# Cross entropy of 256 rows: the first 64 rows read as groups of 16 and 48 rows in place of 8 and 56

## The chip, the cores and the metric

The kernel runs on one core of one Trainium2 chip. The metric is the device time of one execution in microseconds (us). A core has five engines that run side by side and wait for each other through semaphores: TensorE (PE in the profile), VectorE (DVE), ScalarE (ACT), GpSimd (POOL) and SyncE (SP). Here SP does nothing but issue transfers from DRAM; the transfers themselves run on 16 DMA engines. The on-chip memory has 128 partitions, and every compute instruction works on all partitions at once, along the columns of a tile.

## The reference

```python
def setup_inputs():
    batch, num_classes = 256, 32000
    return {
        "logits": np.random.randn(batch, num_classes).astype(np.float32),
        "labels": np.random.randint(0, num_classes, size=batch).astype(np.int32),
    }

def reference(logits, labels):
    log_probs = logits - np.max(logits, axis=-1, keepdims=True)
    log_probs = log_probs - np.log(np.sum(np.exp(log_probs), axis=-1, keepdims=True))
    return np.array([-log_probs[i, labels[i]] for i in range(batch)]).astype(np.float32)
```

For each row the result is log(sum of exp(x)) - x[label]. The logits are 256 x 32,000 floats, 32.77 MB, and every one of them has to be read once and go through one exponential.

## The kernel before

The 256 rows are cut into five groups (`GROUPS`, line 18: 8, 56, 128, 32 and 32 rows). The rows of one group lie one behind the other in DRAM, so a group is one contiguous stretch; `flat` (line 142) cuts this stretch into 128 equal runs, and run p goes to partition p. A group of k rows gives k x 250 columns in each partition. Each group is fetched in one or several loads, cut by columns (`LOADS`, line 20); each load is one transfer issued by SP (`load`, line 213).

Group 0 has 8 rows. It is one load of 2,000 columns, 1 MB, and partition p holds a sixteenth of row p // 16. Group 1 has 56 rows in one load of 14,000 columns: 56 rows don't divide 128 partitions, so a partition's run reaches over row borders, and only pieces of 2,000 columns, seven to a partition, belong to one row each. `span` and `parts` (lines 135 and 136) work this out: with k rows, the run of a partition is cut into k / gcd(k, 128) parts, and 128 / gcd(k, 128) such parts make a row.

`exps` (line 217) runs one exponential on ScalarE for each part of a load, in place. For the loads of the first two groups it also leaves the sum over the columns of each part in `near`. For most later loads (`HALVED`) ScalarE only takes the exponential, and VectorE adds the two halves of the tile and accumulates the sum (line 315).

The sums of a row's pieces lie in different partitions. TensorE adds them: `products` (line 231) multiplies each column of `near` with a 128 x k matrix of weights (`weigh`) that holds, for each row, exp(-x[label]) in the partitions which belong to it and zero elsewhere. The masks `holds` of these partitions are made on GpSimd, with a memset and two selections for each group (lines 274 to 285). The values exp(-x[label]) come from an indirect transfer by the labels (line 268), an exponential on ScalarE placed directly behind load 1's (`GATHERED = 1`, line 290), and a spread over all partitions by TensorE (line 295). VectorE then makes the weights, one product for each part of each group (line 301). The logarithm of a group's row of sums (`logs`, line 239) is the result.

Memory is the reason for the order of loads. There are six slots for loads 0 to 5, whose transfers SP issues one behind the other; the first of them is moved ahead of the barrier at the start of the program. Loads 6 and 7 use the slots of loads 2 and 3 again, so SP waits for VectorE's sums of these. The six loads of the last group, from 2,496 columns down to 608, lie side by side in the slot of load 1. SP issues strictly in this order. ScalarE takes the loads in the order of their numbers. The logarithm of the first two groups stands behind load 2's exponential.

Of the kernel before, what the change touches and what calls it, by code (L numbers as in the profile page):

```python
# [14 lines left out]
AF = mybir.ActivationFunctionType  # L15


GROUPS = [8, 56, 128, 32, 32]

LOADS = [  # L20
    [2000],
    [14000],
    [8896, 8192, 8320, 6592],
    [4736, 3264],
    [2496, 1824, 1344, 992, 736, 608],
# [94 lines left out]
def kernel(  # L120
# [9 lines left out]
    B, C = logits.shape  # L130
    assert B == P * ROWS == sum(GROUPS)
    row_at = [sum(GROUPS[:g]) for g in range(len(GROUPS) + 1)]


    span = [P // math.gcd(k, P) for k in GROUPS]
    parts = [k // math.gcd(k, P) for k in GROUPS]
    for k, ns, n, m in zip(GROUPS, LOADS, span, parts):
        assert sum(ns) * P == k * C and C % n == 0
# [4 lines left out]
        logits[row_at[g]:row_at[g + 1], :].rearrange("k c -> (k c)").rearrange("(p n) -> p n", p=P)  # L143
        for g in range(len(GROUPS))
    ]
# [224 lines left out]
```

## Time and profile before

| | us |
|---|---|
| median of 3 runs (82.7 to 82.85) | 82.72 |
| the profiled execution, its time | 82.85 |
| the profiled execution, its span (first to last instruction) | 81.2 |
| ScalarE busy | 58.5 |
| VectorE busy | 28.5 |
| TensorE busy | 13.0 |
| GpSimd busy | 6.4 |
| bytes moved, mean rate over the span | 32.77 MB, 404 GB/s |

The transfers, as the page lists them: load 1 is the one of 7,000 KB and lands 20.8 us after its issue, load 0 the one of 1,000 KB, with 5.0 us. Loads 2 to 5 are those of 4,448, 4,096, 4,160 and 3,296 KB, with 30.9, 40.1, 49.3 and 56.6 us from issue to landing. All are issued within the first 3.3 us, so these times are mostly time in the queue.

How to read the views: L222 is the exponential, L315 VectorE's sum, L215 the issue of a load, L234 the products of TensorE, L240 the logarithm. ACT is ScalarE and SPq the queue of SP. In the row of slices each character is one fortieth of the span and gives the busy share in tenths. A wait in brackets stands ahead of the instruction that had to wait, with what released it.

### The profile page before, as it was taken

The numbers are of one execution on the slowest core, as the hardware profiler recorded it, in microseconds if no ns is written. First come the engines' busy times: TensorE is split into PE (matmuls) and PEld (weight loads), VectorE is DVE, ScalarE is ACT, GpSimd is POOL, SyncE is SP. The second block draws the span as 40 slices with busy tenths as digits, with TensorE's granted clock in tenths as the row PEclk, the third lists the DMA queues.
The fourth block names the chain that finished last, engine by engine and source line by source line (L and its number), as shares of the span: only waits on it lengthen the run. The fifth ranks groups of instructions, "written<-read, shape, count | busy, mean of one in ns | idle before, by whom it ended". The sixth has DMA issues, their size and how long they took to land.

```text
span 81.2 us, 322 instructions
## 1 busy us (share of the span) xinstructions
PE 13.0 (16%) x80; PEld 7.7 (10%) x80; DVE 28.5 (35%) x37; ACT 58.5 (72%) x35; POOL 6.4 (8%) x22
## 2 busy tenths in 40 slices
PE   0040000000000000067000020020000201159971
PEld 0040000000000000046000000000000000035640
DVE  1010000000000000026019926950099198898870
ACT  6054000000399999999999993599979999999993
POOL 4006982000000000000000000000000000000000
DMA  4999899999989898998998998999999999999930
GB/s 91 532 407 414 386 441 442 441 442 441 491 351 508 368 508 357 436 500 355 436 508 361 443 492 360 416 429 455 392 420 429 426 431 420 423 424 415 405 150 1
DMA packets 2084, 32.77 MB, mean 404 GB/s; under 512 B 290, under 2 KB 291, under 8 KB 1060
## 3 DMA queue, kind: packets, MB, share of 16 engines
q1 hardware_dynamic: 2018, 32.77, 94.8%
q0 software_dynamic: 64, 0.00, 0.1%
q10 hardware_dynamic: 2, 0.00, 0.0%
HBM read 32.77 MB, written 0.00 MB: 404 GB/s over the span
## 4 chain that ended last, share of the span: by engine, by line
DMA 61%; ACT 34%; SPq 2%; another core or an unknown queue 1%; issue 1%; PE 0%
DMA x<-in_logits_dram 61%; ACT x L222 24%; ACT x_tail L222 9%; SPq L215 2%; PE bank L234 0%; ACT res L240 0%
## 5 line engine op out<-in xcount | busy, mean ns | idle before, releaser
L222 ACT ACTIVATE x<-x 128x2000 f32<-128x2000 f32 (+6 forms) x14 | 49.2, 3525 | 20.6 <-DMA x<-in_logits_dram 20.6
L315 DVE SCALAR_TENSOR_TENSOR x<-x 128x4448 f32<-128x4448 f32 (+5 forms) x6 | 21.8, 3631 | 14.1 <-ACT x L222 14.1
L292 DVE TENSOR_SCALAR diag<-ident,eg 128x128 f32<-128x128 f32 x2 | 0.5, 282 | 28.8 <-ACT eg L290 28.8
L234 PE MATMUL bank<-weights,near 128*1 128x32 f32 (+3 forms) x40 | 5.2, 270 | 32.6 <-DVE x L315 31.1
L222 ACT ACTIVATE x_tail<-x_tail 128x2496 f32<-128x2496 f32 (+5 forms) x6 | 7.5, 1302 | 0.0
L295 PE MATMUL bank<-diag,ones 128*128 128x128 f32 x4 | 1.2, 462 | 29.3 <-DVE diag L292 29.3
L312 PE MATMUL bank<-diag,x 128*1 128x128 f32 x32 | 5.8, 368 | 0.0
L234 PEld LDWEIGHTS bank<-weights,near 128*1 128x1 f32 x40 | 2.4, 94 | 35.5 <-DVE x L315 33.4
L315 DVE SCALAR_TENSOR_TENSOR x_tail<-x_tail 128x1248 f32<-128x1248 f32 (+3 forms) x4 | 4.1, 1024 | 0.6 <-ACT x_tail L222 0.3
L295 PEld LDWEIGHTS bank<-diag,ones 128*128 128x128 f32 x4 | 0.9, 323 | 29.4 <-DVE diag L292 29.4
L312 PEld LDWEIGHTS bank<-diag,x 128*1 128x1 f32 x32 | 3.5, 112 | 2.1
L268 POOL DMA_INDIRECT g_at<-in_logits_dram,idx x2 | 2.1, 1030 | 0.6 <-issue 0.3
L207 ACT ACT_TABLE_LOAD x1 | 1.3, 1283 | 0.8 <-PEq L354 0.8
L301 DVE TENSOR_TENSOR weights<-holds,bank 128x56 f32<-128x56 f32 (+3 forms) x11 | 1.4, 204 | 1.2 <-PE bank L295 1.2
L257 PE MATMUL bank<-one,lbl_row 1*128 1x1 f32 x4 | 1.0, 352 | 4.9 <-DVE lbl_row L255 4.9
L255 DVE CAST lbl_row<-words 1x256 f32<-1x256 int32 x1 | 0.3, 281 | 3.5 <-DMA words<-in_labels_dram 3.5
L282 POOL TENSOR_SCALAR_AFFINE_SELECT holds<-holds 128x32 f32<-128x32 f32 (+3 forms) x5 | 1.5, 292 | 0.3
L222 ACT ACTIVATION_READ_ACCUMULATOR x<-x 128x1 f32 x8 | 1.5, 186 | 0.0
L278 POOL TENSOR_SCALAR_AFFINE_SELECT holds<-holds 128x32 f32<-128x32 f32 (+3 forms) x5 | 1.5, 293 | 0.1
L257 PEld LDWEIGHTS bank<-one,lbl_row 1*128 1x128 f32 x4 | 0.9, 318 | 4.9 <-DVE lbl_row L255 4.9
L240 ACT ACTIVATE res<-bank 1x64 f32<-1x64 f32 (+2 forms) x3 | 0.7, 221 | 0.1
L274 POOL MEMSET holds<- 128x592 f32 x1 | 0.6, 606 | 0.0
(15 smaller groups left out, 3.0 us busy)
## 6 DMA issues: line engine op xcount, KB each, us to landing
x<-in_logits_dram SPq DMA_DIRECT2D x1, 7000.0 KB, 20.8
x<-in_logits_dram SPq DMA_DIRECT2D x1, 4448.0 KB, 30.9
x<-in_logits_dram SPq DMA_DIRECT2D x1, 4160.0 KB, 49.3
x<-in_logits_dram SPq DMA_DIRECT2D x1, 4096.0 KB, 40.1
x<-in_logits_dram SPq DMA_DIRECT2D x1, 3296.0 KB, 56.6
x<-in_logits_dram SPq DMA_DIRECT2D x1, 2368.0 KB
x<-in_logits_dram SPq DMA_DIRECT2D x1, 1632.0 KB, 15.1
x_tail<-in_logits_dram SPq DMA_DIRECT2D x1, 1248.0 KB
```

The costliest lines, as they stand in the source:

```text
L207: nc.scalar.preload_act_table_set("natural_log_exp_and_others")
L215: nc.sync.dma_start(out=place[i], in_=flat[GROUP_OF[i]][:, a:a + CHUNKS[i]])
L222: nc.scalar.activation(out=x, in_=x, func=AF.Exp, accum_out=None if i in HALVED else near[i][:, j:j + 1])
L234: nc.tensor.matmul(lane[g], near[i][:, j:j + 1], weigh(g, j), start=i == first_of[g] and j == 0, stop=i == last_of[g] and j == parts[g] - 1,)
L257: nc.tensor.matmul(lbl_up[:, r:r + 1], lbl_row[:, r * P:(r + 1) * P], one[:, :], start=True, stop=True)
L268: nc.gpsimd.indirect_dma_start(out=g_at[:, r:r + 1], out_offset=None, in_=logits[:, :], in_offset=bass.IndirectOffsetOnAxis(ap=idx[:, r:r ...
L278: nc.gpsimd.affine_select(out=h, in_=h, pattern=[[1, m], [-n, k]], base=0, channel_multiplier=m, compare_op=mybir.AluOpType.is_ge, fill=0.0,)
L282: nc.gpsimd.affine_select(out=h, in_=h, pattern=[[-1, m], [n, k]], base=n - 1, channel_multiplier=-m, compare_op=mybir.AluOpType.is_ge, fi ...
L295: nc.tensor.matmul(spread[:, r * P:(r + 1) * P], ones[:, :], diag[r][:, :], start=True, stop=True)
L301: nc.vector.tensor_mul(out=weigh(g, j), in0=holds[:, at:at + k], in1=spread[:, row_at[g]:row_at[g + 1]],)
L312: nc.tensor.matmul(warm, col, diag[0][:, :], start=True, stop=True)
L315: nc.vector.scalar_tensor_tensor(out=place[i][:, 0:half], in0=place[i][:, 0:half], scalar=1.0, in1=place[i][:, half:CHUNKS[i]], op0=mybir. ...
```

## The change

Two constants change; the rest of the code is the same and follows from them.

```diff
-GROUPS = [8, 56, 128, 32, 32]
+GROUPS = [16, 48, 128, 32, 32]
 
 LOADS = [
-    [2000],
-    [14000],
+    [4000],
+    [12000],
     [8896, 8192, 8320, 6592],
     [4736, 3264],
     [2496, 1824, 1344, 992, 736, 608],
```

Load 0 now has 16 rows: 4,000 columns in each partition, one contiguous stretch of 2 MB, an eighth of a row to a partition. Load 1 has 48 rows in 12,000 columns. With gcd(48, 128) = 16 a partition holds three parts of 4,000 columns, and eight parts make a row. So ScalarE runs one exponential of 4,000 columns for load 0 and three for load 1, where it ran one and seven of 2,000. `near` of load 1 has three columns instead of seven; TensorE's products for the first two groups are 1 + 3 instead of 1 + 7, VectorE's weight products 1 + 3 instead of 1 + 7 (48 columns wide instead of 56), and the masks on GpSimd have 16 + 3 x 48 + 192 = 352 columns instead of 8 + 7 x 56 + 192 = 592. The slots of loads 0 and 1 are 4,032 and 12,032 columns wide instead of 2,048 and 14,016, together the same; the other slots, loads, waits and the order of all instructions stay.

## The prediction

> **What bounds the kernel now.** I read the page's slices first: who is busy all the time?
>
> ```profile
> ACT  6054000000399999999999993599979999999993
> DMA  4999899999989898998998998999999999999930
> GB/s 91 532 407 414 386 441 442 441 442 441 491 351 508 368 508 357 436 500 355 436 508 361 443 492 360 416 429 455 392 420 429 426 431 420 423 424 415 405 150 1
> q1 hardware_dynamic: 2018, 32.77, 94.8%
> ```
>
> The transfer engines (DMA row) are full from the second slice to the last but two; ScalarE has a hole of seven slices early and smaller ones later. All 32.77 MB run on one queue. Next I read the chain that ended last, in order of time, to see which of the two sets the end.
>
> ```profile
> 0.80 0.33 SPq L215
> 1.18 0.49 SPq L215
> 1.72 0.55 SPq L215
> 2.31 49.32 DMA x<-in_logits_dram
> 51.65 7.14 ACT x L222
> 59.43 5.63 ACT x L222
> 65.11 3.89 ACT x L222
> 69.17 2.91 ACT x L222
> 72.07 7.46 ACT x_tail L222 x8
> ```
>
> Up to 51.6 us the chain is transfers alone; behind that it is ScalarE's exponentials. The ScalarE timeline tells how the two are joined (columns: start, length, line, tile, and in brackets the idle time ahead and its releaser):
>
> ```profile
> 5.02 1.87 ACT L222 ACTIVATE x<-x 128x2000 f32<-128x2000 f32 x1 [2.93 <-DMA x<-in_logits_dram]
> 21.64 1.87 ACT L222 ACTIVATE x<-x 128x2000 f32<-128x2000 f32 x1 [14.66 <-DMA x<-in_logits_dram]
> ...
> 34.71 7.60 ACT L222 ACTIVATE x<-x 128x8896 f32<-128x8896 f32 x1
> ...
> 42.32 7.01 ACT L222 ACTIVATE x<-x 128x8192 f32<-128x8192 f32 x1
> 51.65 7.14 ACT L222 ACTIVATE x<-x 128x8320 f32<-128x8320 f32 x1 [2.32 <-DMA x<-in_logits_dram]
> 59.43 12.64 ACT L222 ACTIVATE x<-x 128x6592 f32<-128x6592 f32 x3 [0.64 <-DMA x<-in_logits_dram]
> ```
>
> ScalarE waits for data at 51.65 (load 4) and again at 59.43 (load 5). From 59.43 on it never waits again, so the end is the landing of load 5 plus 21.8 us of fixed work (81.2 - 59.4). Loads 0 to 5 are issued at the front with no wait on compute, and they fill the queue until load 5 is in. So what counts is when the last byte of load 5 lands, and nothing on ScalarE before 51.65. The front of the transfers, in half microseconds (last column GB/s; a coarse count, whole pieces are booked to the slice):
>
> ```profile
> 1.00:1.50 0.50, 0.00 (x0) 0.00 (x0) 0.10 (x1) 0.50 (x1) 0.42 (x4) 1.00 1.02 160
> 1.50:2.00 0.50, 0.00 (x0) 0.00 (x0) 0.00 (x0) 0.50 (x1) 0.11 (x1) 1.00 0.80 208
> 2.00:2.50 0.50, 0.00 (x0) 0.00 (x0) 0.00 (x0) 0.09 (x1) 0.00 (x0) 1.00 0.81 336
> 2.50:3.00 0.50, 0.00 (x0) 0.00 (x0) 0.00 (x0) 0.00 (x0) 0.00 (x0) 1.00 1.03 432
> ```
>
> The stream runs up to 432 GB/s over 1.5 us and then stays there (431 from 21.64 to 34.70). Against 432 the ramp loses (272 + 224 + 96) x 0.5 us = 296 KB, or 296/432 = 0.69 us.
>
> **The change, part by part.** The sum is made against the profiled execution: span 81.2 us, time 82.85 us, so 1.65 us lie around it; the median of the runs shown, 82.72, is 0.13 lower, and I apply the difference to the median.
>
> *Bytes ahead of load 5.* Loads 0 and 1 together stay 16,000 columns of 128 partitions, 8.192 MB. Load 5 has the same bytes before it: 0.
>
> *Issues on SP.* Still 14 loads in one order; load 0 is still issued ahead of the barrier, load 1 at 0.80. Load 0 now keeps the engines 2.4 us longer (1.024 MB / 432 GB/s), so load 1's issue has more time to be ready: 0.
>
> *Pieces.* Load 0's 128 runs grow from 8,000 to 16,000 bytes, load 1's shrink from 56,000 to 48,000; their number stays. Does a run's length cost anything here? The nearest row with shorter runs is the tail, 413 GB/s (74 to 76 us, runs of 5 and 4 KB); 1.024 MB at 413 takes 2.48 us, at 432 2.37. So the longer runs are worth between 0 and -0.11 us. Load 0 already shows 432 once it is under way, which is nearest to the first end: I take 0.
>
> *The ramp.* This is the only disputed cost. No row shows a first load with 16,000-byte runs spread over 2 MB. If the slow first stretch goes with the bytes first touched, or with the run length, it doubles: +0.69. If it were to vanish, -0.69. The row is nearest to a delay by the clock: the slow stretch is over by 2.5 us, when (160 + 208 + 336) x 0.5 = 352 KB of load 0's 1,024 have moved, and the rest of the same contiguous stretch runs at full rate. So I take 0 and keep both ends.
>
> The Trainium skill, "DMA: Bandwidth & Descriptors", section "Bandwidth", advises batching transfers to at least 1 MiB and shows efficiency rising with size (341 GB/s at 1 MB, 425 at 16 MB, on another issue path); a reader could conclude that doubling load 0 makes the front faster. By its roughly 2 us of fixed cost for one transfer, 14 serial loads would spend 28 us on it, while the slices here stay near 430 GB/s across every boundary between loads. The fixed part is thus paid once, in the ramp, before and after; by the rule read so the term is also 0, and by the naive reading it would be a gain that no row supports.
>
> *ScalarE.* The step between 2,000-column exponentials is 1.85 us with the accumulator read (30.92 to 32.77). One column costs (7,599 - 7,012) / (8,896 - 8,192) = 0.834 ns, so a 4,000-column one takes 1.85 + 1.67 = 3.52. Load 1: 3 x 3.52 = 10.56 in place of 7 x 1.85 = 12.95, 2.4 us less. Load 0 lands at 5.0 + 2.4 = 7.4 and is done by 10.9; load 1 lands at 21.6 still and is done at 32.2 (before 34.6). Load 2 is there (its issue at 1.18 + 30.9 us to landing = 32.1), so its exponential runs 32.3 to 39.9, then the logarithm of 64 columns. Load 3 lands at 1.72 + 40.1 = 41.8: ScalarE now waits 1.8 us there, runs to 48.8, and waits about 2.8 instead of 2.32 for load 4. 1.8 + 0.5 is, to rounding, the 2.4 saved: all of it becomes waiting, 0 at the end. Without these waits it would be worth -2.4.
>
> *VectorE and TensorE.* Eleven weight products become seven (11 take 1.42 us, so about -0.5) and eight products of the first groups become four (16 recorded matmuls take 1.60, so -0.8). Both ran under load 2's 7.6 us exponential and still do; with that cover gone they would have been 1.3 us. The logarithm behind them waits for nothing: its inputs are ready some 4 us ahead of it.
>
> *GpSimd.* The mask shrinks from 592 to 352 columns and the wide selections from 392 to 144; 0.61 + 2 x 0.56 goes down by about 0.8 us, ending near 12 us without any user before 32: 0. What may come later is the label row: its 2 KB shares the engines with load 0, and its cast starts at 4.59. If it stays behind load 0, it, both gathers and their landing (8.13 + 11.4 = 19.5) slip by up to 2.4 to 21.9. The negated exponential of the gathered values wants them at 32.2, so 10 us remain: 0.
>
> *SP behind a waiting instruction.* Load 6 waits for VectorE's sum of load 2 (issue at 47.17). That comes about 2.4 us earlier; load 7's and the tail's turn 0.5 earlier. The engines are busy with loads 3 to 5 until 59.4 either way: 0.
>
> Sum: 0 on the path, with -0.69 - 0.11 and +0.69 as bounds. Forecast 82.72 us.
>
> **Rivals.** *The ramp grows* (slower): the first run of each engine is twice as long and the 16 engines start over twice the stretch of DRAM; if the loss follows bytes or pages in part, say half, +0.34 gives 83.06, all of it 83.4. Its place is 1.0 to 2.5 us; from a quarter of the loss (0.17 us) on it decides, for nothing between there and the end absorbs it: ScalarE waits for loads 4 and 5, so every later landing goes through. For it: the ramp is real and load 0 is what changes there. Against it: it ends in time while load 0 is still in flight.
>
> *The ramp shrinks* (faster): engines that begin 128,000 instead of 64,000 bytes apart may disturb each other less, and fewer run boundaries fall in the ramp. Half the loss, -0.34, gives 82.38; with the run term too, 82.3. Nothing in the profile ranks it above its opposite, except that the end follows it as closely.
>
> *ScalarE's 2.4 us reach the end* (faster): 80.3. It would need ScalarE to be the bound before 51.65, against two waits in brackets above. *The gathers come too late* (slower): it needs a further 10 us, and 4.6 us of waiting ahead of loads 3 and 4 would absorb the first of it. One in a hundred each.
>
> **How the numbers follow.** A measurement here can tell about 0.2%, 0.17 us, from no change. No change: 0.37, own range 82.55 to 82.89. Ramp grows, 0.35, and with the gathers slower is 0.36. Ramp shrinks, 0.26, with the ScalarE rival faster is 0.27. Slower stands ahead of faster because a first load touching twice the memory is the thing added; the longer runs could gain a tenth. The range cuts both ramp cases at somewhat over half of their bound: 82.35 to 83.15.
>
> **What would show it.** The step of ScalarE's load-1 exponentials should be 3.52 us, with the first start near 7.4 and the second still near 21.6; a new wait of about 1.8 us ahead of the 8,192-column one; starts at 51.65 and 59.43 moved by the same amount as the end. The rate from 1.0 to 2.5 us tells the ramp rivals apart. I am wrong if the 59.43 moves by over 0.17 us with the same ramp, or if the end moves and 59.43 doesn't.

## The result and the profile after

The changed kernel is slower: 83.48 us (median of 4 runs, 83.44 to 83.69) against 82.71 (82.68 to 82.85), a ratio of 1.0095 with a 95% interval of 1.0075 to 1.0115. Its profiled execution took 83.48 us with a span of 81.9, against 82.85 and 81.2. Executions more than 1.5% above the fastest one of the same kernel are left out of the medians and ratios here and below.

The page's slices of the changed kernel, and its one data queue:

```profile
ACT  6000970000099999999929992499969999999993
DMA  6899999998899898999999998999999999999920
GB/s 125 313 439 500 446 446 516 422 422 375 383 435 487 383 487 356 464 464 400 417 471 407 439 455 386 412 477 425 406 426 426 408 421 421 424 420 413 408 88 1
q1 hardware_dynamic: 2018, 32.77, 94.6%
```

The number of pieces and the bytes are what they were. The second slice moved 313 GB/s where it had moved 532, and after that the stream is as full as ever. ScalarE's timeline (start, length; in brackets the wait ahead):

```profile
8.12 3.54 ACT L222 ACTIVATE x<-x 128x4000 f32<-128x4000 f32 x1 [6.04 <-DMA x<-in_logits_dram]
22.41 3.54 ACT L222 ACTIVATE x<-x 128x4000 f32<-128x4000 f32 x1 [10.67 <-DMA x<-in_logits_dram]
25.95 3.52 ACT L222 ACTIVATE x<-x 128x4000 f32<-128x4000 f32 x1
...
33.08 7.60 ACT L222 ACTIVATE x<-x 128x8896 f32<-128x8896 f32 x1
...
42.56 7.03 ACT L222 ACTIVATE x<-x 128x8192 f32<-128x8192 f32 x1 [1.78 <-DMA x<-in_logits_dram]
52.37 7.14 ACT L222 ACTIVATE x<-x 128x8320 f32<-128x8320 f32 x1 [2.78 <-DMA x<-in_logits_dram]
60.16 12.61 ACT L222 ACTIVATE x<-x 128x6592 f32<-128x6592 f32 x3 [0.65 <-DMA x<-in_logits_dram]
```

Load 1 starts 22.41 - 21.64 = 0.77 later than before, load 4 52.37 - 51.65 = 0.72, load 5 60.16 - 59.43 = 0.73, and the span ends 0.7 later. So the whole loss exists when load 1 lands, to within 0.1 us nothing is added or won back behind it, and load 0's own landing already has it: it comes 8.12 - 5.02 = 3.10 us later, of which 2.4 are its additional megabyte. The front of the transfers, in half microseconds (last column GB/s, counted by whole pieces, which begin in the slice):

```profile
1.00:1.50 0.50, 0.00 (x0) 0.00 (x0) 0.10 (x1) 0.50 (x1) 0.42 (x4) 1.00 2.46 448
1.50:2.00 0.50, 0.00 (x0) 0.00 (x0) 0.00 (x0) 0.50 (x1) 0.11 (x1) 1.00 0.38 64
2.00:2.50 0.50, 0.00 (x0) 0.00 (x0) 0.00 (x0) 0.08 (x1) 0.00 (x0) 1.00 1.00 224
2.50:3.00 0.50, 0.00 (x0) 0.00 (x0) 0.00 (x0) 0.00 (x0) 0.00 (x0) 1.00 0.60 256
3.00:3.50 0.50, 0.00 (x0) 0.00 (x0) 0.00 (x0) 0.00 (x0) 0.00 (x0) 1.00 0.68 288
3.50:4.00 0.50, 0.00 (x0) 0.00 (x0) 0.00 (x0) 0.00 (x0) 0.00 (x0) 1.00 0.99 416
```

Before, 432 GB/s stood in the slice from 2.50; now the stream is slow until 3.5 us. The trace's single pieces say the same without that coarseness: an undisturbed run of load 0 takes 302 ns (8,000 bytes) or 596 ns (16,000), but the first sixteen pieces to start took up to 1,214 ns before and 632 to 2,482 ns now. The last piece of load 0 ended at 4.64 us before and at 7.76 now; eight undisturbed pieces one behind the other from 1.03 on would have ended at 3.45 and 5.80. The trace doesn't name the engine of a piece; this takes the 128 pieces as eight for each of the 16 engines. So the slowest engine is 1.20 us behind in the one and 1.96 in the other: 0.76 of difference, which is the loss. I call this the start loss below. Reckoned in the same way up to load 5, the delay stays between 1.20 and 1.27 us before and between 1.89 and 1.98 now: what is lost at the start is carried through.

### The profile page after: what moved, and what is told of

Its sections match the earlier page's. It is cut to its first block, busy times and chain, and to the rows that moved or that the text cites. A ratio compares the mean times of both kernels' runs of the same rounds, so it can differ in the third digit from the quotient of the medians.

```text
span 81.9 us, 290 instructions
## 1 busy us (share of the span) xinstructions
PE 12.2 (15%) x72; PEld 6.9 (8%) x72; DVE 28.0 (34%) x33; ACT 57.8 (71%) x27; POOL 5.8 (7%) x22
## 4 chain that ended last, share of the span: by engine, by line
DMA 61%; ACT 33%; SPq 2%; another core or an unknown queue 1%; issue 1%; PE 0%
DMA x<-in_logits_dram 61%; ACT x L222 24%; ACT x_tail L222 9%; SPq L215 2%; PE bank L234 0%; ACT res L240 0%
## 5 line engine op out<-in xcount | busy, mean ns | idle before, releaser
L222 ACT ACTIVATE x<-x 128x4000 f32<-128x4000 f32 (+6 forms) x10 | 48.5, 4863 | 21.9 <-DMA x<-in_logits_dram 21.9
L234 PE MATMUL bank<-weights,near 128*1 128x32 f32 (+3 forms) x32 | 4.3, 259 | 35.7 <-DVE x L315 34.3
L234 PEld LDWEIGHTS bank<-weights,near 128*1 128x1 f32 x32 | 1.5, 83 | 38.6 <-DVE x L315 36.5
L301 DVE TENSOR_TENSOR weights<-holds,bank 128x48 f32<-128x48 f32 (+3 forms) x7 | 0.9, 201 | 1.2 <-PE bank L295 1.2
L282 POOL TENSOR_SCALAR_AFFINE_SELECT holds<-holds 128x32 f32<-128x32 f32 (+3 forms) x5 | 1.2, 245 | 0.3
L278 POOL TENSOR_SCALAR_AFFINE_SELECT holds<-holds 128x32 f32<-128x32 f32 (+3 forms) x5 | 1.2, 247 | 0.1
L222 ACT ACTIVATION_READ_ACCUMULATOR x<-x 128x1 f32 x4 | 0.7, 186 | 0.0
```

The costliest lines, as they stand in the source:

```text
L222: nc.scalar.activation(out=x, in_=x, func=AF.Exp, accum_out=None if i in HALVED else near[i][:, j:j + 1])
L234: nc.tensor.matmul(lane[g], near[i][:, j:j + 1], weigh(g, j), start=i == first_of[g] and j == 0, stop=i == last_of[g] and j == parts[g] - 1,)
L278: nc.gpsimd.affine_select(out=h, in_=h, pattern=[[1, m], [-n, k]], base=0, channel_multiplier=m, compare_op=mybir.AluOpType.is_ge, fill=0.0,)
L282: nc.gpsimd.affine_select(out=h, in_=h, pattern=[[-1, m], [n, k]], base=n - 1, channel_multiplier=-m, compare_op=mybir.AluOpType.is_ge, fi ...
L301: nc.vector.tensor_mul(out=weigh(g, j), in0=holds[:, at:at + k], in1=spread[:, row_at[g]:row_at[g + 1]],)
```

## The experiments

All edits are to the kernel before unless said; times are medians, ratios are to the kernel before on the same chip, with 95% intervals. "Pitch" is the distance in DRAM between the runs of neighbouring partitions in load 0. Each load has 128 runs, so run length and load size go together. The kernel before took 82.73, 82.70, 82.74, 82.86 and 82.80 us beside the five sets of runs, which follow in this order: load 0 cut by columns; longer and graded runs; wide pitch and control; addresses in the changed kernel; addresses in the kernel before. So times of different sets differ by up to 0.16 us for that reason alone, and the ratio is the fairer number. It isn't always the quotient of the two medians, but that lies within its interval.

**Cutting load 0 by columns.** Four versions with other first loads; where a load is added, the indices that count loads move by one, and the label row goes to GpSimd's queue.

```diff
-GROUPS = [8, 56, 128, 32, 32]
+GROUPS = [16, 48, 128, 32, 32]
 LOADS = [
-    [2000],
-    [14000],
+    [2000, 2000],
+    [12000],
...
-        nc.scalar.dma_start(
+        nc.gpsimd.dma_start(
             out=words[:, :], in_=bass.AP(tensor=lbl_words, offset=0, ap=[[2 * B, 1], [1, 2 * B]])
```

> Groups of 16 and 48 as in the changed kernel, but load 0 cut by columns into two loads of 2,000 columns: runs of 8,000 bytes as in the kernel before, at the changed kernel's pitch of 16,000 bytes (so the 16 DMA engines start 128,000 bytes apart). The label row is fetched by GpSimd's queue instead of ScalarE's, so that the number of transfers on the hardware queues stays a multiple of eight; it has 10 us of slack. Theory RUN (the slow start grows with the length of the first runs; load 0's last piece ended 4.64 us with 8,000 bytes and 7.76 with 16,000, against 3.45 and 5.80 with every piece at its usual duration): the loss is back at that of before, the time about 82.7, the 6,592-column exponential starts near 59.4. Theory STRETCH (it grows with the distance between the places in DRAM where the engines start): 83.4 to 83.5, start near 60.1.

83.11 us, 1.0041 (1.0025 to 1.0058): between the two theories.

```diff
 LOADS = [
-    [2000],
+    [1000, 1000],
     [14000],
```

> Groups of 8 and 56 as before, load 0 cut by columns into two loads of 1,000 columns: runs of 4,000 bytes at the old pitch of 8,000. Label row on GpSimd's queue. RUN, taken as linear through the two points (1.20 us of loss at 8,000 bytes, 1.96 at 16,000): loss 0.8, time about 82.3, 6,592-column exponential near 59.0. STRETCH: as before, 82.7 and 59.4.

83.71 us, 1.0122 (1.0094 to 1.0150): about a microsecond slower, which neither theory had. ScalarE's timeline of this run shows where:

```profile
3.60 1.04 ACT L222 ACTIVATE x<-x 128x1000 f32<-128x1000 f32 x1 [1.51 <-DMA x<-in_logits_dram]
...
4.84 1.04 ACT L222 ACTIVATE x<-x 128x1000 f32<-128x1000 f32 x1
...
22.35 1.87 ACT L222 ACTIVATE x<-x 128x2000 f32<-128x2000 f32 x1 [16.38 <-DMA x<-in_logits_dram]
```

Both halves of load 0 are in by 4.84, ahead of the 5.02 of before, but load 1, whose bytes, addresses and pieces are exactly those of before, lands at 22.35 instead of 21.64. In the trace its first pieces took up to 3,376 ns, where 2,067 is the rule. Behind undisturbed pieces, the slowest engine was 0.99 us late when load 0's halves were in (1.20 before) and 1.89 when load 1 was in (1.27 before). The front can lose a second time, here 0.9 us at the start of load 1.

```diff
-GROUPS = [8, 56, 128, 32, 32]
+GROUPS = [32, 32, 128, 32, 32]
 LOADS = [
-    [2000],
-    [14000],
+    [2000, 6000],
+    [8000],
```

> Groups of 32 and 32; loads of 2,000, 6,000 and 8,000 columns: the first load has runs of 8,000 bytes at a pitch of 32,000, the engines start 256,000 bytes apart. Label row on GpSimd's queue. RUN: as before, 82.7. STRETCH: beyond the changed kernel, 84 or more if linear (0.77 us for each doubling or more).

82.77 us, 1.0003 (0.9990 to 1.0016). RUN has this right, and a distance that costs more the wider it gets is ruled out.

```diff
-GROUPS = [8, 56, 128, 32, 32]
+GROUPS = [4, 60, 128, 32, 32]
 LOADS = [
-    [2000],
-    [14000],
+    [1000],
+    [15000],
```

> Groups of 4 and 60 rows, loads of 1,000 and 15,000 columns: runs of 4,000 bytes at a pitch of 4,000, the engines start 32,000 bytes apart; 14 loads and the label row as before. RUN and STRETCH both: a loss of about 0.8 us, time about 82.3. No theory of the start (the 0.77 us come from something behind load 0): 82.7.

84.87 us, 1.022 (1.0154 to 1.0287), the slowest of all. Where the time goes shows in ScalarE's timeline (of an execution of 85.39 us):

```profile
3.41 1.04 ACT L222 ACTIVATE x<-x 128x1000 f32<-128x1000 f32 x1 [1.33 <-DMA x<-in_logits_dram]
...
24.02 1.04 ACT L222 ACTIVATE x<-x 128x1000 f32<-128x1000 f32 x1 [19.48 <-DMA x<-in_logits_dram]
```

Load 0's own start loss is 0.78 us, as both theories foretold (its last piece ended at 3.04, eight undisturbed ones of 155 ns from 1.01 on would have ended at 2.25). The rest is lost at load 1, which lands at 24.02 instead of 21.64: its pieces took up to 3,311 ns, where 2,221 is the rule. So the shorter first runs do lose less here, but the kernel isn't better for it, and neither theory has the second loss.

**Longer and graded runs.** I then held that the engines, all started together, hinder each other as long as they are in step (theory STEP). The edits are again only in the first rows of `GROUPS` and `LOADS`.

```diff
+GROUPS = [32, 32, 128, 32, 32]   LOADS = [[4000, 4000], [8000], ...
```

> Groups of 32 and 32, loads of 4,000, 4,000 and 8,000 columns (label row on GpSimd's queue, as in the 2,000/6,000/8,000 version that took 82.77): the first runs are 16,000 bytes again, at a pitch of 32,000. Theory STEP (while the 16 engines are still in step each run is slow in proportion to its length; the delays pull them apart and the rest runs at full rate): as the changed kernel, loss of load 0 near 1.96 us, time 83.4 to 83.5. Theory STRETCH (distance in DRAM): the loss goes with the pitch, so like the 2,000/6,000/8,000 version at the same pitch, 82.8. A rival that blames the size of load 0 (2 MB) says 83.4 too; the fourth kernel and the earlier second-load losses speak to it.

83.15 us, 1.0057 (1.0042 to 1.0071): between STEP and STRETCH, and 0.38 above the 2,000/6,000/8,000 version at the same pitch, as the changed kernel is 0.37 above its split version (83.48 and 83.11); by the ratios it is 0.45 in both pairs. In these pairs twice the run length costs about 0.4 at either pitch.

```diff
+GROUPS = [32, 32, 128, 32, 32]   LOADS = [[8000], [8000], ...
```

> Groups of 32 and 32, loads of 8,000 and 8,000 columns, 14 loads and the label row as in the two given kernels: the first runs are 32,000 bytes. STEP, linear through 1.20 us at 8,000 and 1.96 at 16,000: loss 3.5 us, time near 85.0. STRETCH or a fixed loss: between 82.7 and 83.5.

83.39 us, 1.0084 (1.0052 to 1.0115), far below STEP's 85.0 and inside what a fixed loss or STRETCH would give. The loss doesn't grow linearly with the runs.

```diff
+GROUPS = [32, 32, 128, 32, 32]   LOADS = [[1000, 7000], [8000], ...
```

> Groups of 32 and 32, loads of 1,000, 7,000 and 8,000 columns, label row on GpSimd's queue. STEP: load 0 loses 0.8 to 1.0 us, but leaves the engines in step within about 0.5 us, so that the second load's runs of 28,000 bytes lose again, about half of what the 56,000-byte runs lost in the 1,000/1,000/14,000 version (0.9 us of 1.88 in all): some 0.4 us, time 82.8 to 83.1. If the second loss there was due to load 1's long runs alone at its place in DRAM: no second loss, time 82.4.

82.72 us, 1.0003 (0.9982 to 1.0024): below STEP's interval by a little, above the other. In the trace the start loss is 1.33 us when load 0 is in and still 1.33 when the second load is in. So STEP's second loss isn't there, and its time is nearly met by luck: load 0 lost more than the 0.8 to 1.0 foretold.

```diff
+GROUPS = [16, 48, 128, 32, 32]   LOADS = [[1000, 3000], [12000], ...
```

> Groups of 16 and 48, loads of 1,000, 3,000 and 12,000 columns, label row on GpSimd's queue: runs of 4,000, 12,000 and 48,000 bytes. STEP: load 0 loses 0.8 to 1.0, the 12,000-byte runs little (0.1 to 0.2), and by then the engines are apart: loss about 1.1, time 82.6 to 82.8, the best of the versions with the changed groups. A theory that the first 2 MB of the 16-row group lose whatever the cut: 83.1 to 83.5.

82.72 us over seven executions (82.60 to 83.62), 1.0020 (0.9988 to 1.0051); three more took 83.90 to 84.40. That is too scattered to decide, though the median lies in STEP's interval.

**Wide pitch, and a control.** One group of 64 rows makes load 0 a column slice of all of them, at a pitch of 64,000 bytes, with the loads' sizes of the two given kernels, 14 loads and the label row where it was.

```diff
-GROUPS = [8, 56, 128, 32, 32]
+GROUPS = [64, 128, 32, 32]
 LOADS = [
-    [2000],
-    [14000],
+    [2000, 14000],
...
-EARLY = 1
+EARLY = 0
```

> The first 64 rows as one group, loads of 2,000 and 14,000 columns: first runs of 8,000 bytes at a pitch of 64,000; 14 loads and the label row as in the two given kernels. The versions so far read as two prices that add: runs of 16,000 in place of 8,000 bytes cost 0.37 (pitch 16,000) and 0.38 (pitch 32,000), and a pitch of 16,000 costs 0.3 to 0.4 against 8,000 and 32,000. TWO PRICES: 82.7 to 82.8, and 0.37 below the next kernel. CONTIGUITY (load 0 has to be one stretch of DRAM): 83.1 or more.

82.43 us, 0.9953 (0.9937 to 0.9969): faster than both given kernels, against CONTIGUITY, and about 0.3 below the 82.7 of TWO PRICES. ScalarE's timeline of it:

```profile
4.62 1.87 ACT L221 ACTIVATE x<-x 128x2000 f32<-128x2000 f32 x1 [2.54 <-DMA x<-in_logits_dram]
...
21.34 11.87 ACT L221 ACTIVATE x<-x 128x14000 f32<-128x14000 f32 x1 [14.76 <-DMA x<-in_logits_dram]
...
59.08 12.60 ACT L221 ACTIVATE x<-x 128x6592 f32<-128x6592 f32 x3 [0.65 <-DMA x<-in_logits_dram]
```

Load 0 lands 0.40 us earlier than before with the same bytes, load 1 0.30, load 5 0.35.

```diff
+    [4000, 12000],
```

> The same with loads of 4,000 and 12,000 columns: first runs of 16,000 bytes at a pitch of 64,000. TWO PRICES: 83.1. If run length had mattered only because of something in the split versions (the extra load, GpSimd's queue): as the kernel before this one, no difference.

82.56 us, 0.9979 (0.9965 to 0.9993). The changed kernel's own load sizes, into the same slots, are 0.9 us faster here than in it. What run length adds is 0.13 at this pitch (0.2 by the ratios), not 0.37: the two prices don't simply add.

The control moves half of the label row to GpSimd's queue, in either given kernel:

```diff
         nc.scalar.dma_start(
-            out=words[:, :], in_=bass.AP(tensor=lbl_words, offset=0, ap=[[2 * B, 1], [1, 2 * B]])
+            out=words[:, 0:B], in_=bass.AP(tensor=lbl_words, offset=0, ap=[[2 * B, 1], [1, B]])
+        )
+        nc.gpsimd.dma_start(
+            out=words[:, B:2 * B], in_=bass.AP(tensor=lbl_words, offset=B, ap=[[2 * B, 1], [1, B]])
         )
```

> The kernel before with the second half of the label row fetched by GpSimd's queue, the first half still by ScalarE's: a control for the versions that moved the label row. No price of GpSimd's queue: 82.7. If it disturbs the start: above 82.9.

82.74 us, 0.9992 (0.9978 to 1.0006).

> The same control for the changed kernel. No price: 83.4 to 83.5. If part of what the split versions won came from the label row on GpSimd's queue: below 83.3.

83.41 us, 1.0063 (1.0039 to 1.0086). No price in the kernel before. In the changed one the median is within the expectation, but the ratio is 0.003 (0.26 us) below the 1.0095 of the changed kernel, with intervals that overlap; and only half of the row was moved. So the versions that moved the whole row can be read beside the others to 0.1 us at best, and to 0.3 us at worst.

**Load 0's addresses alone.** This was the test that settles most: a given kernel is kept whole, and only the source of load 0 is moved, so that its 128 runs lie further apart. In the changed kernel:

```diff
-        nc.sync.dma_start(out=place[i], in_=flat[GROUP_OF[i]][:, a:a + CHUNKS[i]])
+        src = flat[GROUP_OF[i]][:, a:a + CHUNKS[i]]
+        if i == 0:
+            src = bass.AP(tensor=logits.tensor, offset=0, ap=[[4256, P], [1, CHUNKS[0]]])
+        nc.sync.dma_start(out=place[i], in_=src)
```

with 4,256 floats (17,024 bytes), then 6,000, 8,000 and 16,000.

> The changed kernel with load 0's 128 runs of 16,000 bytes read at a pitch of 17,024 in place of 16,000 bytes (so not contiguous, 2.2 MB wide); the first 16 rows are computed from other data, all else is the same. DISTANCE GROWS (the wider apart the engines start, the smaller the loss): hardly changed, 83.3 to 83.5. CERTAIN DISTANCES (16,000 is a bad one): any value, below 83.2 if a small move leaves the bad one. GROUPS (the 48-row load or the groups are to blame, not load 0's addresses): 83.4 to 83.5 here and in the next three.

83.32 us, 1.0057 (1.0035 to 1.0078): in DISTANCE GROWS' interval, just below that of GROUPS, and not below the 83.2 that leaving a single bad pitch would give. The interval still overlaps with that of the changed kernel, which belongs to another set.

> The same with a pitch of 24,000 bytes; the first 16 rows are computed from other data. DISTANCE GROWS: 83.3. CERTAIN DISTANCES: open, not in order. GROUPS: 83.4 to 83.5.

82.94 us, 1.0027 (1.0008 to 1.0046): 0.4 below DISTANCE GROWS, and against GROUPS.

> The same with a pitch of 32,000 bytes; the first 16 rows are computed from other data. Both distance theories: 83.15, as with the groups of 32 and 32. GROUPS: 83.4 to 83.5.

83.00 us, 1.0027 (1.0008 to 1.0046), no higher than at 24,000. The distance theories took their 83.15 from the 4,000/4,000/8,000 version, whose first load is this very one: the same addresses, the same runs. There the ratio was 1.0057 (1.0042 to 1.0071). ScalarE's first exponential in that version, then in this run:

```profile
7.90 3.54 ACT L222 ACTIVATE x<-x 128x4000 f32<-128x4000 f32 x1 [5.81 <-DMA x<-in_logits_dram]
7.52 3.54 ACT L225 ACTIVATE x<-x 128x4000 f32<-128x4000 f32 x1 [5.43 <-DMA x<-in_logits_dram]
```

The intervals barely overlap. So some 0.25 us by the ratios, and 0.38 in these two executions, come from something that isn't load 0's source: the groups behind it, the label row's queue, the added load and the chip differ too, and no run tells them apart.

> The same with a pitch of 64,000 bytes; the first 16 rows are computed from other data. Both distance theories: 82.6, as with one group of 64 rows. GROUPS: 83.4 to 83.5.

82.73 us, 0.9998 (0.9977 to 1.0020). The theory GROUPS falls: with the groups, the products, the 48-row load and every other load in place, the loss against the kernel before is gone. From ScalarE's timeline of this run (the edit moves the exponential's line from 222 to 225):

```profile
7.28 3.54 ACT L225 ACTIVATE x<-x 128x4000 f32<-128x4000 f32 x1 [5.20 <-DMA x<-in_logits_dram]
...
21.57 3.54 ACT L225 ACTIVATE x<-x 128x4000 f32<-128x4000 f32 x1 [10.66 <-DMA x<-in_logits_dram]
...
59.30 12.64 ACT L225 ACTIVATE x<-x 128x6592 f32<-128x6592 f32 x3 [0.64 <-DMA x<-in_logits_dram]
```

Load 0 lands at 7.28 instead of 8.12, load 1 at 21.57 instead of 22.41, load 5 at 59.30 instead of 60.16: 0.84, 0.84 and 0.86 us.

The same edit in the kernel before, with 4,000 and with 16,000 floats:

> The kernel before with load 0's 128 runs of 8,000 bytes read at a pitch of 16,000 in place of 8,000 bytes; the first 8 rows are computed from other data. DISTANCE GROWS: at or below the kernel before. CERTAIN DISTANCES (16,000 is a bad pitch for any run): 0.3 to 0.4 above it, as the split version with the same pitch. If the split version's extra came from its second load: no difference.

83.23 us, 1.0052 (1.0034 to 1.0070). Moving 1 MB of source addresses makes the kernel before 0.43 us slower (83.23 against 82.80); its timeline:

```profile
5.49 1.87 ACT L225 ACTIVATE x<-x 128x2000 f32<-128x2000 f32 x1 [3.40 <-DMA x<-in_logits_dram]
...
22.07 1.87 ACT L225 ACTIVATE x<-x 128x2000 f32<-128x2000 f32 x1 [14.63 <-DMA x<-in_logits_dram]
...
59.83 12.64 ACT L225 ACTIVATE x<-x 128x6592 f32<-128x6592 f32 x3 [0.64 <-DMA x<-in_logits_dram]
```

0.47 us at load 0, 0.43 at load 1 and 0.40 at load 5.

> The same at a pitch of 64,000 bytes; the first 8 rows are computed from other data. Both: 0.3 below the kernel before, as one group of 64 rows.

82.62 us, 0.9979 (0.9968 to 0.9991): faster by 0.18, not by 0.3.

The kernels that differ from a given one in load 0's addresses alone, side by side:

| runs of load 0 | pitch 8,000 | 16,000 | 17,024 | 24,000 | 32,000 | 64,000 |
|---|---|---|---|---|---|---|
| 8,000 bytes (kernel before) | 1 | 1.0052 | | | | 0.9979 |
| 16,000 bytes (changed) | | 1.0095 | 1.0057 | 1.0027 | 1.0027 | 0.9998 |

The start loss in the traces goes the same way. In the order of the table it is 1.20, 1.68 and 1.04 us in the first row, and 1.96, 1.89, 1.29, 1.36 and 1.12 in the second.

## Why the prediction was wrong

The forecast was no change, and 83.48 lies above its range. The direction and the place were those of the rival "the ramp grows", and the price was 0.77 us, a little more than the whole of its bound (0.69), not half.

*The step that failed* is the ramp: "The row is nearest to a delay by the clock ... So I take 0." The rate table of before showed that the slow stretch ended at 2.5 us, while load 0 was still under way; from this I concluded that it didn't depend on load 0's shape. One profile can't tell a clock from a cause that ends by itself. Nor is the ramp a fixed part, the same before and after, as the prediction also concludes: the start loss was 1.04 to 1.68 us in the one kernel and 1.12 to 1.96 us in the other when load 0's addresses alone were moved. The runs put in its place that the start loss depends on where load 0's runs lie and how long they are. Of the 0.77 us, 0.43 come with the pitch of 16,000 bytes alone (1.0052). The rest, about 0.35 (1.0095 against 1.0052), comes with runs of twice the length at that pitch, which is also a load of twice the size; the two pairs of versions that double the runs at one pitch agree with about 0.4. But at 32,000 it would be 0.2 with the run in which load 0's addresses alone were moved (1.0027 against 1.0003), and at 64,000 the same doubling costs 0.1 to 0.2.

*The bounds were built on the wrong quantity.* The 0.69 was what all engines together lost against 432 GB/s. ScalarE starts only behind load 0's last piece (0.38 us behind it before, 0.36 now), so the slowest engine counts, and that one was 1.20 us behind before and 1.96 now. A bound from load 0's landing would have been +1.2, and a range built on it could have held the result. The ends of the range were then cut at somewhat over half of the bounds without a row for it.

*Right:* the end follows the landing of load 5 one to one (0.73 there, 0.7 at the end). The exponentials step by 3.52 us, as computed; load 2's begins at 33.08 and not 32.3, which is the late landing of load 1. The new wait ahead of the 8,192-column exponential is 1.78 (1.8 foretold) and the one ahead of load 4 2.78 (2.8). So ScalarE's saving did turn into waiting, wholly. TensorE's busy time fell by 0.8 and VectorE's by 0.5, as worked out; GpSimd's by 0.6 instead of 0.8. The cast of the labels moved from 4.59 to 6.29, 1.7 of the allowed 2.4, with no effect.

*The rule on large transfers.* The naive reading, a faster front through a larger first load, was set aside rightly but for an insufficient reason. The table of the Trainium skill, "DMA: Bandwidth & Descriptors", section "Bandwidth", gives efficiency by size alone; in these runs the same kernel with the same first load of 2 MB takes 1.0095 or 0.9998 of the time of the kernel before, according to the addresses of that load.

## What stays open

Why a pitch of 16,000 is the bad one isn't settled. At runs of 8,000 bytes both 8,000 and 64,000 are better than it, so neither "wider is better" nor "contiguous is better" holds throughout; with 16,000-byte runs the loss falls as the pitch widens, apart from 24,000 and 32,000, which can't be told apart, and neighbouring values overlap in their intervals. Nor is it shown what the engines share in these microseconds. The prediction and several expectations reckon with the distance between the places where the engines start (128,000 in place of 64,000 bytes); no trace shows which runs an engine takes, and what the runs vary is the pitch alone. Load 0's source isn't everything either: the same first load at a pitch of 32,000 gave 1.0057 and 1.0027, and at 64,000, with 8,000-byte runs, 0.9953 in the one group of 64 rows and 0.9979 in the kernel before. The loss of load 1 behind first runs of 4,000 bytes (the 1,000/1,000/14,000 version, and groups of 4 and 60) is measured, not explained, and the 1,000/7,000/8,000 version doesn't have it; that the engines are too much in step is a guess which its linear form did not survive.

## What to carry to other kernels

Where a stream of transfers sets the end, the landing of the first load is part of every execution: read it as the slowest engine's delay against an undisturbed stream, not from the mean rate, and treat the first load's source addresses and run length as parameters to be measured. To find such a cause, keep the kernel whole and move one load's source alone, even if some rows are then computed from other data. Here a first load taken as a column slice of 64 rows, 8,000 bytes out of every 64,000, beats both kernels: 82.43 us, 0.9953 (0.9937 to 0.9969). About half of that gain comes with load 0's addresses (0.9979 when they alone are moved); the other half isn't explained.

## What the runs showed of the hardware

Moving the source addresses of one megabyte, a thirty-second of the data, changed the time by +0.43 or -0.18 us, all of it before load 0 is in (ScalarE starts on it 0.47 us later or 0.19 earlier). From load 2 on the undisturbed pieces take the same time in every run (33,280 bytes in 1,232 ns, which over 16 engines is 432 GB/s), whatever the start. A stream that had settled near full rate (408 to 416 GB/s from 2.0 to 3.5 us) lost again when the next load began: 0.9 us at load 1 in the 1,000/1,000/14,000 version, in transfers that lost under 0.1 us in the kernel before.

The Trainium skill, "DMA: Bandwidth & Descriptors", section "Latency and other measured facts", reports lower rates for row pitches of large powers of two, with channels that collide as its inferred cause. None of the pitches here is such a power, and the loss here ends by itself; that pitch matters agrees, that the cause is the same no run shows.
